# The last feed-forward's gate and up as block products: 20 f-tiles in seven products instead of eight, with weight sums on GpSimd

## The chip, the cores and the metric

The kernel runs on one core of a Trainium2 chip. The metric is the device time of one launch in microseconds; the median of several runs is given. Six parts of the core matter here: TensorE (PE in the rows; its weight loads are PEld), VectorE (DVE), ScalarE (ACT), GpSimd (POOL), SyncE (SP), which issues the DMAs, and the 16 DMA engines.

## The reference, cut to what matters

Three transformer layers over 512 tokens of width 1024, in float32. The change touches only the last feed-forward, at the end of the third layer:

```python
# second_block; D_MODEL = 1024, D_FF_2 = 2816, h is (1, 512, 1024)
u = rmsnorm(h, norm2_w[l]) * (1.0 + sc2) + sh2
ff = (jax.nn.silu(u @ w_ffn_gate[l]) * (u @ w_ffn_up[l])) @ w_ffn_down[l]
h = h + g2 * ff
...
return rmsnorm(h, final_norm_w)
```

## The kernel before

Features lie on the 128 partitions and the 512 tokens on the columns, so a product of a 128 x 128 weight tile with a k-tile of the operand gives 128 outputs x 512 tokens, one PSUM bank. A float32 product is made of three float32r matmuls (`mm3`, L533): weight high part x operand high part, high x low, low x high; a high part is a cast on ScalarE (`whi`, `xh`, `ph`), a low part the difference on VectorE (`wlo`, `xl`, `pl`).

The weights come as one stream in the order of `weight_plan` (L57): 16 tiles of 128 x 128 make a unit of 1 MB, loaded by one DMA of SyncE (`load_unit`, L424) into one of `RAWBUFS` = 2 raw buffers `wraw`. A unit is split in two halves of 1024 columns (`prep_half`, L477; `finish`, L443) into rings of three `whi` and three `wlo` tiles. The next unit is loaded when both halves of the one in its buffer are split (`load_ahead`, L469).

Code is emitted by a planner written out by hand (`Core.run`, L354): generators are threads with priorities, the planner keeps a clock for every engine from its own prices, and a thread runs when what it waits for is there by these clocks. The order on each engine is the order of emission; at run time every engine works through its own list in that order, and semaphores hold an instruction until its operands are made or its target is free.

The last feed-forward is `ffn("F2", ...)` (L862). There are 22 f-tiles of 128 hidden features, in two halves of 11; each half is followed by its part of the down product (8 output tiles of 11 k-tiles). The first f-tile's gate and up and the second one's gate are one wide product (`gemm_wide`, L555): three outputs side by side, first over tokens 0 to 255, then 256 to 511, while the operand is still being made by `explicit_x` (L1389). That one makes `ut` from the norm, then `xh` on ScalarE and `xl` on VectorE, for every third k-tile on GpSimd. Every other f-tile is a gate product and an up product (`gemm_a`, L541), 8 k-tiles of 3 matmuls of 512 columns each, then `act_chain` (L865): Silu on ScalarE into `fs`, multiply on VectorE, split into `ph` and `pl`, the operand of the down product. `update` (L598) adds a down product to `h`.

## Time and profile before

| | us |
|---|---|
| three runs | 1958.1, 1958.9, 1957.89 |
| median | 1958.1 |
| span of the profiled execution | 1956.9 |
| TensorE busy | 1940.5 |
| VectorE busy | 1139.1 |
| ScalarE busy | 843.1 |
| GpSimd busy | 7.0 |

The last feed-forward takes the end of the span: the wide product ends at 1595 us, the first half's gate and up at 1701, the second half's run from 1761 to 1885. The rows that are quoted further down have times in microseconds from the start of the span. A matmul is named by what it writes and reads (`ps<-xh,whi`), by its weight tile (128*128), and by partitions x columns; matmuls overlap, so their pitch is read from the starts. A bracket behind a row is the idle time of the engine ahead of it and what ended it. The granted TensorE clock is given as a share of 2.4 GHz.

### The profile page before, as it was taken

The page shows a single profiled execution, that of the slowest core. Times are in us where ns is not written, and L with a number is a line of the kernel's source. Part 1 is how long each engine was busy: PE and PEld are TensorE (multiplying, and loading weights), DVE is VectorE, ACT ScalarE, POOL GpSimd, SP SyncE. Part 2 cuts the span into 40 slices and gives each one's busy share as a digit, 9 for nine tenths or more (in the row PEclk, how much of TensorE's full clock was granted, in tenths as well). Part 3 has the DMA queues.
Part 4 walks back from the last instruction along what each step waited for, and adds up shares of the span by engine and source line. Part 5 has one row for each costly group of instructions (what it writes and reads, how often), then busy time and mean ns, then how long its engine had stood idle before and what let it go on. Part 6 is the DMA issues. An engine that isn't in the chain of part 4 may idle for free.

```text
span 1956.9 us, 23731 instructions
## 1 busy us (share of the span) xinstructions
PE 1940.5 (99%) x9331; PEld 1593.4 (81%) x9331; DVE 1139.1 (58%) x1946; ACT 843.1 (43%) x1361; POOL 7.0 (0%) x14
## 2 busy tenths in 40 slices
PE   9999999999999999999999999999999999999998
PEld 6888888888778878878888888898888888888887
DVE  5877865655665578887443344474777563333334
ACT  4866743322333466665322223352546352212233
POOL 0000000000000000000000000000000000000000
PEclk9999999999999999999999999999999999999999
DMA  6333224544442344431322222222121222222221
GB/s 192 99 85 97 76 86 176 194 178 172 185 170 86 123 130 128 126 114 65 108 94 99 87 108 87 104 84 97 54 82 44 87 87 86 99 95 89 106 86 65
DMA packets 48303, 211.94 MB, mean 108 GB/s; under 512 B 7056, under 2 KB 10304, under 8 KB 29248
## 3 DMA queue, kind: packets, MB, share of 16 engines
q1 hardware_dynamic: 48192, 210.43, 31.7%
q8 instruction: 73, 1.20, 0.2%
q14 instruction: 38, 0.31, 0.0%
HBM read 186.26 MB, written 2.10 MB: 96 GB/s over the span
## 4 chain that ended last, share of the span: by engine, by line
PE 96%; DVE 2%; DMA 1%; ACT 1%; issue 0%; SPq 0%; POOLq 0%; POOL 0%; DVEq 0%; ACTq 0%
PE ps L229 94%; PE ps L235 2%; DMA wraw<-wst 0%; DVE wlo L260 0%; DMA h<-xT 0%; DVE xl L276 0%; ACT xh L242 0%; DVE ut L276 0%; SPq L298 0%; ACT whi L242 0%; DVE h L260 0%; ACT sqh L242 0%; ACT ut L242 0%; DVE h L276 0%; DVE e L276 0%
## 5 line engine op out<-in xcount | busy, mean ns | idle before, releaser
L229 PE MATMUL ps<-xh,whi 128*128 128x512 f32 (+1 forms) x1856 | 728.7, 393 | 3.5 <-ACT whi L242 2.0
L229 PE MATMUL ps<-xh,wlo 128*128 128x512 f32 (+1 forms) x1856 | 722.4, 389 | 0.5 <-DVE wlo L260 0.5
L229 PE MATMUL ps<-xl,whi 128*128 128x512 f32 (+1 forms) x1856 | 719.3, 388 | 2.1 <-POOL xl L264 1.9
L242 ACT ACTIVATE whi<-wraw 128x1024 fp32r<-128x1024 f32 (+1 forms) x280 | 290.8, 1039 | 626.3 <-PE ps L229 579.6
L260 DVE TENSOR_TENSOR wlo<-wraw,whi 128x1024 fp32r<-128x1024 f32 (+1 forms) x280 | 335.6, 1199 | 337.1 <-ACT whi L242 334.3
L229 PEld LDWEIGHTS ps<-xh,whi 128*128 128x128 f32 x1856 | 348.8, 188 | 82.0 <-ACT whi L242 3.8
L229 PEld LDWEIGHTS ps<-xl,whi 128*128 128x128 f32 x1856 | 348.9, 188 | 80.6 <-POOL xl L264 2.9
L229 PEld LDWEIGHTS ps<-xh,wlo 128*128 128x128 f32 x1856 | 348.4, 188 | 78.8 <-DVE wlo L260 1.6
L229 PE MATMUL ps<-ph,whi 128*128 128x512 f32 (+1 forms) x572 | 214.2, 374 | 0.0
L229 PE MATMUL ps<-pl,whi 128*128 128x512 f32 (+1 forms) x572 | 213.3, 373 | 0.0
L229 PE MATMUL ps<-ph,wlo 128*128 128x512 f32 (+1 forms) x572 | 213.2, 373 | 0.0
L229 PEld LDWEIGHTS ps<-ph,wlo 128*128 128x128 f32 x572 | 107.7, 188 | 19.1
L229 PEld LDWEIGHTS ps<-ph,whi 128*128 128x128 f32 x572 | 107.7, 188 | 19.0
L229 PEld LDWEIGHTS ps<-pl,whi 128*128 128x128 f32 x572 | 107.7, 188 | 18.9
L260 DVE TENSOR_TENSOR fu<-ps,rb 128x512 f32<-128x512 f32 x44 | 30.4, 690 | 102.5 <-PE ps L229 102.5
L260 DVE TENSOR_TENSOR h<-ps,h 128x512 f32<-128x512 f32 (+1 forms) x82 | 49.8, 621 | 61.9 <-PE ps L229 59.8
L242 ACT ACTIVATE fs<-fg 128x512 f32<-128x512 f32 x44 | 27.8, 631 | 91.0 <-DVE fg L260 91.0
L260 DVE TENSOR_TENSOR fs<-ps,fs 128x512 f32<-128x512 f32 x22 | 15.2, 692 | 73.7 <-PE ps L229 73.0
L242 ACT ACTIVATE ph<-fs 128x512 fp32r<-128x512 f32 x66 | 41.8, 633 | 28.8 <-DVE fs L260 28.8
L276 DVE SCALAR_TENSOR_TENSOR adacc<-adaw,sc,adacc 128x1024 f32<-128x1024 f32 x42 | 53.7, 1279 | 0.0
L242 ACT ACTIVATE e<-e 128x1024 f32<-128x1024 f32 (+1 forms) x48 | 41.3, 905 | 21.7 <-DVE e L269 21.6
L242 ACT ACTIVATE s<-s,md 128x256 f32<-128x256 f32 (+3 forms) x80 | 45.9, 585 | 9.8 <-DVE md L269 8.4
(211 smaller groups left out, 1977.6 us busy)
## 6 DMA issues: line engine op xcount, KB each, us to landing
wraw<-wst SPq DMA_DIRECT2D x148, 1024.0 KB, 4.7
adaw<-wada SPq DMA_DIRECT2D x48, 512.0 KB, 5.7
qhh<-hin SPq DMA_DIRECT2D x32, 128.0 KB, 2.4
rfs<-rf SPq DMA_DIRECT2D x64, 64.0 KB, 2.0
khh<-rf SPq DMA_DIRECT2D x32, 128.0 KB, 2.5
h<-xT SPq DMA_DIRECT2D x8, 256.0 KB, 4.9
kst<-hin SPq DMA_DIRECT2D x16, 128.0 KB, 2.4
kst<-qkf SPq DMA_DIRECT2D x16, 128.0 KB, 2.4
```

The lines of the kernel that those rows point to most:

```text
L229: self.nc.tensor.matmul(out, lhsT, rhs, start=start, stop=stop, skip_group_check=not group)
L235: self.nc.tensor.transpose(out, in_, ident)
L242: self.nc.scalar.activation(out, in_, func, **kw)
L260: self.nc.vector.tensor_tensor(out, a, b, op)
L276: self.nc.vector.scalar_tensor_tensor(out, a, s, b, op0, op1)
```

## The change

From the third f-tile on (9 in the first half, 11 in the second) gate and up of one f-tile are one product of blocks. The 16 weight tiles of an f-tile are one unit: its four blocks of 512 columns are a11 (gate, k-tiles 0 to 3), a12 (gate, 4 to 7), a21 (up, 0 to 3) and a22 (up, 4 to 7). The operand has four blocks as well: k-tiles 0 to 3 and 4 to 7, tokens 0 to 255 (c1) and 256 to 511 (c2). Instead of eight block products there are seven, by Winograd's form of Strassen's scheme, with the weight blocks a11, a12, a22 and the sums s1 = a21 + a22, s2, s3 and s4. A block product is 4 k-tiles x 3 passes of 256 columns, 12 matmuls, so an f-tile has 84 of 256 columns instead of 48 of 512.

The sums of weight blocks are four GpSimd additions of 128 x 512 for each f-tile (`sums`), three of them in place in the raw unit. Seven blocks are split (cast on ScalarE, difference on VectorE) with 512 columns each into a ring of ten slots (`split_highs`, `split_lows`): six are the old `whi` and `wlo`, now one tile of six slots each, four are new (`whx`, `wlx`). The operand's blocks and their sums are made once (`blocks`): 16 GpSimd additions of 256 columns that put high and low part together again, sums and differences on VectorE (`d00` and so on), and their high and low parts (`th`, `tl`, and in `xh`, `xl` in place). The outputs are put together in `chain`: copies out of PSUM on ScalarE, additions on VectorE, then Silu, multiply and split as before. Product s2 is written into the bank that holds a11 and a12, and so waits for the flag c1, which an addition on VectorE sets; s3, a22 and s4 wait for c2, c3 and c4.

Besides, there are three raw buffers instead of two, the stream is filled up to whole units ahead of the third layer and behind each down product of the last feed-forward, and the DMA descriptors' scratch has a size of its own. The planner's work is the same elsewhere, but the third buffer shifts some of its order in layer 1.

```diff
-RAWBUFS = 2
+RAWBUFS = 3
...
+    def fill():
+        while len(tiles) % UNIT:
+            tiles.append(None)
+    def ffn(g, u, d, wide=False, seven=False):
         for half in range(2):
             for f in range(half * HALF, (half + 1) * HALF):
                 if wide and f == 0:
                     wide_k((g, 0), (u, 0), (g, P))
                     continue
+                if seven and f > 1:
+                    sevens.append(len(tiles) // UNIT)
                 if not wide or f != 1:
                     form_a(g, [f])
                 form_a(u, [f])
             form_a(d, range(8), nk=HALF, k0=half * HALF)
+            if seven:
+                fill()
...
     ffn("w_gate1", "w_up1", "w_down1")
+    fill()
...
+    ffn("w_ffn_gate_2", "w_ffn_up_2", "w_ffn_down_2", True, True)
...
+    hi_slots = wpool.tile([P, 6, 512], FR, name="whi")
+    lo_slots = wpool.tile([P, 6, 512], FR, name="wlo")
+    slots = [(hi_slots[:, i, :], lo_slots[:, i, :]) for i in range(6)]
...
+    EARLY = 2
+    BLOCK = {"a11": 0, "a12": 1, "a21": 2, "a22": 3, "s3": 2, "s2": 0, "s4": 1}
...
+    def steps_of(n):
+        steps = [(x, f) for f in range(EARLY) for x in ("a11", "a12")]
+        steps += [(x, f) for x in ("s1", "s2", "s3") for f in range(EARLY)]
+        steps += [(x, f) for f in range(EARLY - 1) for x in ("a22", "s4")]
+        for f in range(EARLY, n - 1):
+            steps += [("a11", f), ("a12", f), ("s1", f), ("s2", f), ("a22", f - 1), ("s4", f - 1), ("s3", f)]
+        f = n - 1
+        steps += [("a11", f), ("a12", f), ("s1", f), ("s2", f), ("a22", f - 1), ("s3", f), ("s4", f - 1), ("a22", f),
+                  ("s4", f)]
+        return steps
...
+        g["ring"] = [first, first + 1, *more, *((first + x) % 6 for x in range(2, 6))]
...
+    def sums(u0):
+        g = groups[u0]
+        for f in range(g["n"]):
+            u = u0 + f
+            if u not in raw:
+                yield lambda: u in raw
+            if f >= 2:
+                yield from got(f"W{u - 2}s1")
+            t = g["s1"][u] = g["pool"].tile([P, 512], FT, name="s1", bufs=2)
+            b = [raw[u][:, i * 512:(i + 1) * 512] for i in range(4)]
+            yield E._ready("pool_t", [t], b[2:]) - 1.0
+            E.ptt(t, b[2], b[3], OP.add)
+            E.set(f"W{u}S1")
+            yield from got(*(f"W{u}{x}" for x in (("a11", "a12") if f else ())))
+            if not f:
+                while highs.get(2 * u) or lows.get(2 * u):
+                    yield lambda: not (highs.get(2 * u) or lows.get(2 * u))
+            E.ptt(b[2], b[0], b[2], OP.add)
+            E.set(f"W{u}S3")
+            yield E.pool_t - 1.0
+            E.ptt(b[0], t, b[0], OP.add)
+            E.set(f"W{u}S2")
+            yield E.pool_t - 1.0
+            E.ptt(b[1], b[0], b[1], OP.add)
+            E.set(f"W{u}S4")
...
+    def seven(u0, name, f, out, x, fresh):
+        g, u = groups[u0], u0 + f
...
+        else:
+            yield from E.get(f"W{u}{name}x")
+            hi, lo = slots[g["slot"][name, f]]
+        for j in range(4):
+            c = slice(j * P, (j + 1) * P)
+            a, b = yield from x(j)
+            yield from E.there(hi[:, c], lo[:, c], a, b)
+            mm3(out, (hi[:, c], lo[:, c]), (a, b), fresh and j == 0, True, T // 2, False)
+            yield
+        taken[g["slot"][name, f]] = None
...
+    def ffn_seven(tag, pool, explicit, upd, split=False):
+        n = T // 2
+        c1, c2 = HALVES
+        tt = [pool.tile([P, 3, 4, n], FR, name=f"t{x}") for x in "hl"]
...
+        def blocks(j):
+            b = {}
+            for t in range(2):
+                for k in (j, j + 4):
+                    yield from E.get(f"{tag}x{k}_{t}")
+                    b[k // 4, t] = value[k][:, t, :]
+                    c = HALVES[t]
...
+                    d = E.ptt(b[k // 4, t], xh[:, k, c].bitcast(FT), xl[:, k, c].bitcast(FT), OP.add, n=n)
+            u, e, q, v = made[j][0][:, 0, :], made[j][0][:, 1, :], made[j][1][:, 0, :], made[j][1][:, 1, :]
+            def split(hi, lo, t, flag):
+                yield max(E.act_t - SLACK, E._ready("act_t", [hi], [t]))
+                yield E.act(hi, t, AF.Copy, n=n)
+                E.set(f"{tag}x{flag}{j}", E.tt(lo, t, hi.bitcast(FT), OP.subtract, n=n))
+            def minus(hi, lo, t, flag):
+                yield max(E.act_t - SLACK, E._ready("act_t", [hi], [t]))
+                yield E.act(hi, t, AF.Copy, scale=-1.0, n=n)
+                E.set(f"{tag}x{flag}{j}", E.stt(lo, t, -1.0, hi.bitcast(FT), OP.mult, OP.subtract, n=n))
+            yield d
+            E.tt(e, b[1, 1], b[0, 1], OP.subtract, n=n)
+            yield E.tt(u, b[0, 0], b[0, 1], OP.subtract, n=n)
+            E.spawn(after(f"{tag}k{j}", split(xh[:, j, c2], xl[:, j, c2], u, "s1")), 5)
+            yield E.tt(q, b[0, 0], e, OP.add, n=n)
+            E.spawn(minus(tt[0][:, 0, j, :], tt[1][:, 0, j, :], q, "s2"), 6)
+            yield E.tt(v, q, b[1, 0], OP.subtract, n=n)
+            E.spawn(split(tt[0][:, 1, j, :], tt[1][:, 1, j, :], e, "s3"), 8)
+            yield from split(tt[0][:, 2, j, :], tt[1][:, 2, j, :], v, "a22")
...
+        def chain(half, u, f, a, r5):
+            r = ps[:, a, c1]
+            yield from E.get(f"W{u}pa12")
+            g = pool.tile([P, T], FT, name="fs", bufs=3)
+            v = pool.tile([P, n], FT, name="fv", bufs=3)
+            d = E.act(g[:, c1], r, AF.Copy, n=n)
+            yield d
+            d = E.tt(g[:, c1], ps[:, a, c2], g[:, c1], OP.add, n=n)
+            E.set(f"W{u}c1", d)
+            yield d
+            E.act(g[:, c1], g[:, c1], AF.Silu, n=n)
+            yield from E.get(f"W{u}ps2")
+            E.set(f"W{u}c2", E.act(g[:, c2], r, AF.Copy, n=n))
+            yield from E.get(f"W{u}ps3")
+            d = E.act(v, r, AF.Copy, scale=-1.0, n=n)
+            E.set(f"W{u}c3", d)
+            yield d
+            b = yield from got(f"W{u}ps1")
+            E.set(f"W{u}c4", E.tt(v, v, ps[:, r5[0], c1], OP.subtract, n=n))
+            yield from E.get(f"W{u}pa22")
+            E.stt(g[:, c1], r, -1.0, g[:, c1], OP.mult, OP.mult, n=n)
+            E.release([a])
+            yield from E.get(f"W{u}ps4")
+            d = E.tt(g[:, c2], ps[:, r5[0], c1], g[:, c2], OP.add, n=n)
+            E.release([r5[0]])
+            yield d
+            yield E.act(g[:, c2], g[:, c2], AF.Silu, n=n)
+            d = E.tt(g[:, c2], g[:, c2], v, OP.mult, n=n)
+            if half:
+                yield from E.get(f"{tag}d{f}")
+            yield d
+            if not half:
+                hold(f)
...
+            for name, f in groups[u0]["steps"]:
+                u = u0 + f
+                f += 0 if half else 2
+                if name == "a11":
+                    a = (yield from E.alloc())[0]
+                    banks[f] = [a, []]
+                    E.spawn(chain(half, u, f, a, banks[f][1]), 4)
+                elif name == "s1":
+                    banks[f][1] += yield from E.alloc()
+                before = {"s2": "c1", "s3": "c2", "a22": "c3", "s4": "c4"}.get(name)
+                if before:
+                    yield from E.get(f"W{u}{before}")
+                a, r5 = banks[f]
+                out = {"a12": (a, c2), "s1": (r5, c1), "s4": (r5, c1)}.get(name, (a, c1))
+                b = out[0][0] if isinstance(out[0], list) else out[0]
+                yield from seven(u0, name, u - u0, ps[:, b, out[1]], operand(name), name in ("a11", "s1"))
+                E.set(f"W{u}p{name}", E.now())
...
+        skip_to_unit()
...
+            yield from ffn_seven("F2", pool, True, down("Z", x=False, scale=mod_col(5)), split=True)
...
+    nc = bacc.Bacc("TRN2", target_bir_lowering=False, num_devices=1, dynamic_dma_scratch_size=1024)
...
```

**How the order moves.** VectorE in the second half, around the f-tile whose hidden tile is number 4. Before, an f-tile has two weight splits of 1024 columns, the multiply (`fs`) and the hidden tile's low part (`pl`):

```order
L260 TENSOR_TENSOR wlo_13598<-wraw_13513,whi_13597 128x1024
L260 TENSOR_TENSOR fs_13630<-ps_69,fs_13630 128x512
L260 TENSOR_TENSOR wlo_13626<-wraw_13513,whi_13625 128x1024
L260 TENSOR_TENSOR pl4_12125<-fs_13630,ph4_12114 128x512
L260 TENSOR_TENSOR wlo_13661<-wraw_13576,whi_13660 128x1024
L260 TENSOR_TENSOR fs_13693<-ps_69,fs_13693 128x512
```

After, from the addition behind s4 of one f-tile (`fs_13904`, with the PSUM operand) to the addition that sets c1 of the f-tile two further on (`fs_14142`):

```order
L269 TENSOR_TENSOR fs_13904<-ps_69,fs_13904 128x256
L269 TENSOR_TENSOR wlo_85<-wraw_13931,whi_84 128x512
L269 TENSOR_TENSOR fs_13904<-fs_13904,fv_13905 128x256
L269 TENSOR_TENSOR fv_14024<-fv_14024,ps_69 128x256
L269 TENSOR_TENSOR wlo_85<-s1_13995,whi_84 128x512
L269 TENSOR_TENSOR pl4_12487<-fs_13904,ph4_12486 128x512
L269 TENSOR_TENSOR wlo_85<-wraw_13931,whi_84 128x512
L269 TENSOR_TENSOR fs_14142<-ps_69,fs_14142 128x256
```

The splits are half as wide and more, and ahead of the addition that s2 waits for stand the splits of a12, of s1 and of s2 of the next f-tile and the low part of the hidden tile of the one before.

GpSimd in the same place; before, nothing of GpSimd stands there. After, two f-tiles' units:

```order
L273 TENSOR_TENSOR s1_13995<-wraw_13931 128x512
L273 TENSOR_TENSOR wraw_13931<-wraw_13931 128x512
L273 TENSOR_TENSOR wraw_13931<-s1_13995,wraw_13931 128x512
L273 TENSOR_TENSOR wraw_13931<-wraw_13931 128x512
L273 TENSOR_TENSOR s1_14114<-wraw_14050 128x512
L273 TENSOR_TENSOR wraw_14050<-wraw_14050 128x512
```

In a unit's four rows come s1, s3, s2 and s4, the last three in place, so s3 and s2 follow the splits of the blocks that they write over.

VectorE at the end of the wide product, where the last operands are made. Before:

```order
L276 SCALAR_TENSOR_TENSOR ut_12339<-ps_69,gv_83,h_70 128x256
L260 TENSOR_TENSOR wlo_12309<-wraw_11902,whi_12308 128x1024
L276 SCALAR_TENSOR_TENSOR xl_72<-ut_12339,mod_77,xh_71 128x256
L276 SCALAR_TENSOR_TENSOR ut_12346<-ps_69,gv_83,h_70 128x256
L276 SCALAR_TENSOR_TENSOR xl_72<-ut_12346,mod_77,xh_71 128x256
L260 TENSOR_TENSOR wlo_12352<-wraw_12076,whi_12351 128x1024
L260 TENSOR_TENSOR fs_12387<-ps_69,fs_12387 128x512
```

After, to the low part of the last operand (`xl_72<-ut_11891`):

```order
L285 SCALAR_TENSOR_TENSOR xl_72<-ut_11882,mod_77,xh_71 128x256
L285 SCALAR_TENSOR_TENSOR ut_11891<-ps_69,gv_83,h_70 128x256
L269 TENSOR_TENSOR d01_11659<-b0_11650,d00_11658 128x256
L269 TENSOR_TENSOR d10_11660<-b5_11655,b1_11651 128x256
L269 TENSOR_TENSOR d10_11660<-b1_11651 128x256
L269 TENSOR_TENSOR d01_11659<-d01_11659,b4_11654 128x256
L269 TENSOR_TENSOR wlo_85<-wraw_11442,whi_84 128x1024
L269 TENSOR_TENSOR wlx_11649<-wraw_11612,whx_11648 128x512
L269 TENSOR_TENSOR d20_11662<-b6_11656,b2_11652 128x256
L269 TENSOR_TENSOR d20_11662<-b2_11652 128x256
L269 TENSOR_TENSOR d11_11661<-b1_11651,d10_11660 128x256
L285 SCALAR_TENSOR_TENSOR xl_72<-ut_11891,mod_77,xh_71 128x256
```

Two weight splits and seven steps on the operand's blocks now stand ahead of the last operand's low part; before, the low part followed its `ut` at once.

ScalarE at the end of the second half, where the down product's first weights are split. Before:

```order
L242 ACTIVATE whi_13940<-wraw_13828 128x1024
L242 ACTIVATE ph9_12119<-fs_13945 128x512
L242 ACTIVATE whi_13975<-wraw_13891 128x1024
L242 ACTIVATE fs_14008<-ps_69 128x512
L242 ACTIVATE whi_14003<-wraw_13891 128x1024
L242 ACTIVATE ph10_12120<-fs_14008 128x512
L242 ACTIVATE whi_14038<-wraw_13954 128x1024
```

After (`fs_14497` and `ph9` belong to the last f-tile but one, `fs_14609` and `ph10` to the last):

```order
L251 ACTIVATE fs_14609<-ps_69 128x256
L251 ACTIVATE fs_14609<-fs_14609 128x256
L251 ACTIVATE fs_14609<-ps_69 128x256
L251 ACTIVATE fv_14610<-ps_69 128x256
L251 ACTIVATE fs_14497<-fs_14497 128x256
L251 ACTIVATE ph9_13080<-fs_14497 128x512
L251 ACTIVATE whi_84<-wraw_14407 128x1024 x2
L251 ACTIVATE whi_84<-wraw_14542 128x1024
L251 ACTIVATE fs_14609<-fs_14609 128x256
```

The first casts of the down weights (1024 columns) now follow `ph9`; before, they were spread between the last f-tiles' steps.

## Rows read from the trace of the kernel before

**Rows 1.** Page, parts 1 and 4: engines' busy time, chain of waits by engine.

```profile
PE 1940.5 (99%) x9331; PEld 1593.4 (81%) x9331; DVE 1139.1 (58%) x1946; ACT 843.1 (43%) x1361; POOL 7.0 (0%) x14
...
PE 96%; DVE 2%; DMA 1%; ACT 1%; issue 0%; SPq 0%; POOLq 0%; POOL 0%; DVEq 0%; ACTq 0%
```

**Rows 2.** Windows of both gate-and-up stretches: start:end, length, busy by engine, clock, DMA.

```profile
1600.80:1701.40 100.60, 100.60 (x433) 80.93 (x432) 33.71 (x36) 28.40 (x36) 0.00 (x0) 1.00 0.27 96
1761.20:1884.20 123.00, 123.00 (x529) 98.95 (x528) 40.63 (x43) 34.20 (x43) 0.00 (x0) 1.00 0.26 94
```

**Rows 3.** Timeline (start, duration, engine, operation): TensorE, first and last of 528.

```profile
1761.37 0.40 PE L229 MATMUL ps<-xh,whi 128*128 128x512 f32 x1
...
1884.58 0.40 PE L229 MATMUL ps<-ph,whi 128*128 128x512 f32 x1
```

**Rows 4.** Timeline of TensorE at the end of the wide product.

```profile
1592.09 0.28 PE L229 MATMUL ps<-xh,wlo 128*128 128x256 f32 x1
...
1594.00 0.28 PE L229 MATMUL ps<-xh,whi 128*128 128x256 f32 x1
...
1595.09 0.39 PE L229 MATMUL ps<-xh,whi 128*128 128x512 f32 x1
```

**Rows 5.** Lines by form: operation, count | busy us, mean ns | idle before, releasers.

```profile
L242 ACT ACTIVATE whi<-wraw 128x1024 fp32r<-128x1024 f32 x272 | 287.6, 1058 | 625.7 <-PE ps L229 579.6 <-issue 42.6 <-DMA wraw<-wst 2.5
L242 ACT ACTIVATE ph<-fs 128x512 fp32r<-128x512 f32 x66 | 41.8, 633 | 28.8 <-DVE fs L260 28.8
L242 ACT ACTIVATE wh<-ps 128x256 fp32r<-128x256 f32 x20 | 7.6, 381 | 0.5 <-PE ps L229 0.5
L242 ACT ACTIVATE xh<-ut 128x256 fp32r<-128x256 f32 x8 | 3.3, 418 | 0.3
L260 DVE TENSOR_TENSOR wlo<-wraw,whi 128x1024 fp32r<-128x1024 f32 x272 | 332.2, 1222 | 336.9 <-ACT whi L242 334.1 <-PE ps L229 1.0
L260 DVE TENSOR_TENSOR h<-ps,h 128x256 f32<-128x256 f32 x20 | 7.3, 415 | 5.4 <-PE ps L229 3.7 <-PE ps L235 1.8
```

**Rows 6.** Timeline of VectorE: a split of 512 columns and the operation behind it.

```profile
403.80 0.68 DVE L260 TENSOR_TENSOR pl<-fs,ph 128x512 fp32r<-128x512 f32 x1
404.41 1.22 DVE L260 TENSOR_TENSOR adal<-adacc,adah 128x1024 fp32r<-128x1024 f32 x1
```

**Rows 7.** Timeline of GpSimd and VectorE while the last feed-forward's operand is made.

```profile
1581.76 0.73 POOL L264 TENSOR_TENSOR xl<-ut,xh 128x256 fp32r<-128x256 f32 x1 [3.30 <-ACT xh L242]
...
1582.55 0.48 DVE L276 SCALAR_TENSOR_TENSOR xl<-ut,mod,xh 128x256 fp32r<-128x256 f32 x1
...
1586.89 0.74 POOL L264 TENSOR_TENSOR xl<-ut,xh 128x256 fp32r<-128x256 f32 x1 [4.40 <-ACT xh L242]
1587.18 0.72 DVE L276 SCALAR_TENSOR_TENSOR xl<-ut,mod,xh 128x256 fp32r<-128x256 f32 x1 [1.19 <-ACT xh L242]
...
1590.01 1.21 DVE L260 TENSOR_TENSOR wlo<-wraw,whi 128x1024 fp32r<-128x1024 f32 x1
1590.93 0.88 POOL L264 TENSOR_TENSOR xl<-ut,xh 128x256 fp32r<-128x256 f32 x1 [3.30 <-ACT xh L242]
1591.22 0.87 DVE L276 SCALAR_TENSOR_TENSOR xl<-ut,mod,xh 128x256 fp32r<-128x256 f32 x1
```

**Rows 8.** Timeline of ScalarE and VectorE: the wide product's last operand.

```profile
1592.52 0.51 ACT L242 ACTIVATE xh<-ut,mod 128x256 fp32r<-128x256 f32 x1 [1.34 <-DVE ut L276]
1592.94 1.04 ACT L242 ACTIVATE whi<-wraw 128x1024 fp32r<-128x1024 f32 x1
1593.07 0.48 DVE L276 SCALAR_TENSOR_TENSOR xl<-ut,mod,xh 128x256 fp32r<-128x256 f32 x1 [0.58 <-ACT xh L242]
```

**Rows 9.** Page, part 6: a weight unit's DMA, count, KB, median us to landing.

```profile
wraw<-wst SPq DMA_DIRECT2D x148, 1024.0 KB, 4.7
```

**Rows 10.** Windows of the first 100 us and of a stretch of layer 1.

```profile
0.00:100.00 100.00, 95.95 (x462) 74.31 (x463) 69.74 (x93) 65.68 (x96) 0.52 (x5) 1.00 0.49 147
1200.00:1300.00 100.00, 98.81 (x549) 85.69 (x548) 51.25 (x87) 39.80 (x62) 2.30 (x3) 1.00 0.25 89
```

More of the change, by code (lines that the diff above doesn't have):

```diff
@@ L59, in weight_plan @@
     gains = {}
+    sevens = []
     def gain(name, width, i0):
@@ L901, in ffn @@
             last = KT - 2 if half and split else KT
+            for m in range(last):
+                b = yield from E.alloc()
+                hook = (lambda k: E.set(f"{tag}d{k}", E.now())) if m == KT - 1 else None
+                yield from gemm_a(b[0], take(HALF), lambda k: (ph[k], pl[k]), nk=HALF,
+                                  need=f"{tag}p{half}_" if m == 0 else None, hook=hook)
+                E.spawn(upd(m, b[0], half), 3)
+            if last == KT:
+                continue
+            i = take((KT - last) * HALF)
```

188 lines of the change are left out of this document (173 added, 15 removed).

## The prediction

> **What bounds the kernel now.** I read the page's busy shares and chain first: TensorE is busy 1940.5 us of a span of 1956.9 us and holds 96% of the chain that ended last [rows 1]. In the stretches by stage, the two gate-and-up stretches of the last feed-forward show no microsecond without TensorE, at a granted clock of 1.00 (the 2.4 GHz level), while VectorE and ScalarE are busy a third of the time and GpSimd not at all [rows 2]. So nothing but matmul time is to be won there, and what the change adds to the other engines is free only as long as it stays behind the matmuls.
>
> How fast matmuls follow each other comes from the timeline. In the second half's gate and up, 11 f-tiles of 48 matmuls of 512 columns start between 1761.37 and 1884.58 us [rows 3]: 123.21 / 528 = 0.2334 us each, 11.20 us for an f-tile. Matmuls of 256 columns, each with its own weights and the next operand already there, start 25 between 1592.09 and 1595.09 us [rows 4]: 0.1200 us each, more than half of 0.2334.
>
> **The saving.** Each of 20 f-tiles (9 in the first half, 11 in the second) loses its 48 wide matmuls and gets 7 products of 4 k-tiles and 3 passes, 84 matmuls of 256 columns: 84 x 0.1200 = 10.08 us. That is 1.12 us less, **22.4 us** in all. The same rate is the first thing to check in the new trace.
>
> **What the other engines get.** Per f-tile VectorE has seven low splits of 512 columns, one for the hidden tile, five 256-column steps. Back to back, 512 columns take it 0.61 us (403.80 to 404.41) [rows 6], 256 columns 0.42 alone [rows 5], in a row some 0.35 (less the 0.07 between 0.68 and 0.61): about 6.7 us. ScalarE gets eight casts at 0.63, three PSUM copies at 0.38 and two Silus at 0.42 [rows 5]: 7.0 us. GpSimd gets four sums of 512 columns. Its only row of that kind is 256 columns in 0.73 us [rows 7]; 512 lie between 0.73 + 0.43 = 1.16 (only the reading grows) and 1.46. I take 1.16, since the next paragraph shows the reading apart from the rest; 4.6 us. None of these fills 10.08 us.
>
> **The port.** But VectorE and GpSimd do not run beside each other freely. A VectorE operation with two operands in SBUF takes 0.48 us undisturbed and 0.72 us when issued 0.29 us after a GpSimd sum began; behind a 1024-column split, and with a GpSimd sum issued 0.29 us ahead of it, it takes 0.87 us, and the GpSimd sum itself 0.88 instead of 0.73 [rows 7]. One waits for the other. In the first case VectorE is let in 0.53 us after the sum began (1587.18 + 0.24 - 1586.89), in the second it loses 0.39: GpSimd keeps it out for about 0.43 us in 256 columns. For 512 the bounds are 0.43 and 0.86; both operands are read to the end, so I take 0.86. That a VectorE step with one operand in PSUM is not held off is assumed. Per f-tile, eight and a half VectorE operations (5.2 us) and four sums (3.4 us) share that way in: 8.6 of 10.08 us. It fits on average; the places where it must not be late are the question.
>
> The Trainium skill speaks against this change here. Its page "SBUF — State Buffer", section "Who interferes with whom", says that a VectorE instruction with two SBUF inputs contends with a GpSimd instruction that reads SBUF, and that the winner keeps the shared pair for the whole instruction. The trace agrees on the contention (0.72 for 0.48), but not on the whole instruction: 0.43 of 0.73 us. What the whole would cost is the slower rival.
>
> **Term C, the wait inside each f-tile.** The product s2 adds to the bank that holds a11 and a12, so it waits until these were taken out (ScalarE, then an add on VectorE, the last of the rows of VectorE's order). Only s1 lies between: 12 x 0.12 = 1.44 us. Unhindered it is enough: tail of a matmul 0.16 (0.28 less 0.12), copy 0.38, add 0.42, hand-overs of 0.04 (ScalarE's end at 1593.03 to VectorE at 1593.07) [rows 4, 5, 8]: 1.1 us. Hindered: take time zero at the end of a12. The slot for the split of a12 two f-tiles on is free after four products, 5.76 + 0.20; cast 0.63, low split 0.68 with 0.3 behind GpSimd's sum s2: over at 7.6. From there, in VectorE's order, come the multiply (0.35), the split of s1, the hidden tile's and the split of s2 (0.61 each), and GpSimd, freed by that same a12 split, puts s4, and s1 and s3 of the next unit, between them (0.86 each): 4.76 us through one door, until 12.36. The add must be issued at 10.08 + 1.44 - 0.46 = 11.06: 1.3 us late. If the third sum loses to the split of s2, 0.86 less: 0.4 late. In [rows 7] the one that waited first got in, which speaks for 1.3; a tenth or two in GpSimd's hand-overs turns it round. I take the mean, 0.86, on the 11 f-tiles whose add has two later sums ahead of it: **+9.5 us**, bounds 0 and 14. Behind the waiting add stand the splits of the f-tile's own a22 and s4, eight products ahead of TensorE, so they cost nothing. The unit that feeds these sums lands 4.7 us after its issue [rows 9], at about 8 us, before GpSimd asks for it.
>
> **Term A, the end of the wide product.** Now the last operand follows its ScalarE cast at once (1592.52, 1593.07), and only then the split of the next half starts (1592.94) [rows 8]; TensorE uses it at 1594.00. The new order puts, ahead of that cast, a 1024-column cast that waits for TensorE to have passed k-tile 5, and two of 512; and on VectorE a 1024 split, a 512 split and seven small steps ahead of the operand's low part. From the start of k-tile 5: three matmuls, their tail and a hand-over 0.56 + 1.06 + 1.22 + 0.61 + three steps 1.0 + 0.48 = 4.9, against 2.16 us of matmuls for k-tiles 5 and 6: 2.7 us at least. The operand sums on GpSimd add up to 0.9 at k-tile 5 (a 1024 split holds its low part off) and 0.9 more at the end. I take **+4 us**, bounds 2.7 and 5.
>
> **Term B, the first two f-tiles.** From the last operand to the second f-tile's add, VectorE has 12 operations of 512 and 24 of 256 columns: 12 x 0.61 + 24 x 0.36 = 16 us, in 16.8 us of matmuls (up of f-tile 1, 5.6; seven products, 10.1; 1.1 before). Alone it just fits. Seven sums and one operand sum of GpSimd in that time keep it out for 6.4 us, 5.6 too many. Nearly all its operations there have two SBUF operands, so nearer the upper end: **+4 us**, bounds 0 and 6.
>
> **Term D, the ends of both groups.** The order of ScalarE puts the first split of the down weights behind the hidden tile of the last f-tile but one. From the end of that tile's s4: 0.16 + add 0.42 + Silu 0.42 + multiply 0.42 + cast 0.63 + split 1.06 and 1.22, hand-overs 0.2: 4.5 us, with two products (2.88) left. 1.6 us, twice: **+3 us**, bounds 1 and 4.
>
> The rest at nothing, with 2 us either way: a third raw buffer and half a unit of empty tiles shift the order of layer 1's attention; TensorE idles 4.1 us in the first 100 and 1.2 us in the stretch from 1200 to 1300 [rows 10], so little is to be gained outside.
>
> **The sum.** -22.4 + 9.5 + 4 + 4 + 3 = -1.9 us. The profiled execution spans 1956.9 us; the median of the three runs is 1958.1, 1.2 above, which I take for what lies around a span. 1956.9 + 1.2 - 1.9 = **1956 us**: the saving is real and nearly all of it is given back in waits.
>
> **Rivals.**
> *The port decides nothing (faster).* GpSimd's sums fall into VectorE's gaps, so C and B are 0, and A and D stay at 2.7 and 3. For it: 8.6 of 10.08 us, and splits stand eight products ahead. Against: the stretched rows [rows 7], and the add at the end of the queue. 1958.1 - 22.4 + 5.7 = 1941 us.
> *GpSimd keeps VectorE out longer (slower).* If a 512-column sum holds it off for its whole 1.16 us, each of the three sums ahead of the add costs 0.3 more: 2.2 us late, x 11 = 24; B 8, A 5, D 3: 40 against 22.4, 1976 us. It decides from a hold of some 0.9 us on: there C passes 1.04 us for an f-tile and the sum turns positive. By the page named above this is what happens. Against it: 0.43 of 0.73 us.
> *It does not do what it says.* At 11.20 / 84 = 0.133 us for a narrow matmul no product is won and the waits stay: 1958.1 + 20.5 = 1979 us. Against it 0.1200 over 25 matmuls beside a working VectorE [rows 4, 8].
>
> **How the numbers follow.** My forecast (C between its two orders, 1948 to 1965) has 0.55, the faster rival 0.23, the slower 0.17, the last 0.05. A measurement of this kernel can tell 0.2% (3.9 us) from no change: below 1954.2 is faster, above 1962 slower. The forecast's 0.55 splits 0.17 faster, 0.30 same, 0.08 slower. So faster 0.40, same 0.30, slower 0.30. The range runs from the faster rival's time to short of the slower one's: 1941 to 1970, with about 0.07 below and 0.13 above left out.
>
> **What would show it.** Narrow matmuls 0.120 apart in products, and nearly no gap but ahead of s2, ended by VectorE's add, 0.4 to 1.3 us in 11 f-tiles; low splits of 0.68 us stretched to over 1 beside GpSimd; GpSimd sums near 1.2 us; 4 us of gap before the wide product's last k-tile, 4 in the first seven products after it, 1.6 before each down product, ended by the split. Adds on time, or sums of 1.5 us and more, would make it wrong, as would a gap ended by GpSimd itself.

## The result, and the profile after

The changed kernel takes 2001.5 us (median of 4 runs, 1997.1 to 2004.1) against 1958.0 for the kernel before (4 runs): a ratio of 1.0218, 95% interval 1.0203 to 1.0232. It is slower by 43.5 us where 2 us less were forecast, outside the range of 1941 to 1970. The profiled execution spans 2002.4 us, 45.5 more than before's.

The page's parts 1 and 4 of the changed kernel answer to [rows 1], and the two gate-and-up stretches to [rows 2]:

```profile
PE 1944.6 (97%) x10051; PEld 1636.3 (82%) x10051; DVE 1281.9 (64%) x2156; ACT 910.1 (45%) x1555; POOL 138.9 (7%) x110
...
PE 86%; DVE 8%; issue 2%; ACT 1%; DMA 1%; POOL 1%; SPq 0%; DVEq 0%; ACTq 0%; POOLq 0%
```

```profile
1600.80:1702.00 101.20, 84.37 (x590) 81.52 (x591) 84.40 (x117) 48.80 (x105) 46.60 (x33) 0.88 0.21 74
1781.00:1898.00 117.00, 100.18 (x712) 97.04 (x711) 94.94 (x111) 52.59 (x109) 60.16 (x40) 0.90 0.21 73
```

Two things are new in the second fence. TensorE, without a gap before, is idle for 17 us of each stretch, and its granted clock is 0.88 and 0.90 where it was 1.00. TensorE's waits from 1570 to 1900 us (total us, times, longest) say for whom, first before and then after:

```profile
PE ps L229 <- POOL xl L264: 1.0, 3, 0.4
```

```profile
PE ps L238 <- DVE fs L269: 27.4, 14, 4.2
PE ps L238 <- DVE xl L285: 10.6, 2, 10.0
PE ps L238 <- POOL xl L273: 1.2, 3, 0.4
```

The addition that sets c1 (`fs`) and the wide product's last operand (`xl`): the two places that the prediction named. The steady state on TensorE, in the second half; each row is the first matmul of an s2:

```profile
1829.13 0.39 PE L238 MATMUL ps<-th,whx 128*128 128x256 f32 x1 [1.93 <-DVE fs L269]
...
1842.88 0.39 PE L238 MATMUL ps<-th,whi 128*128 128x256 f32 x1 [1.93 <-DVE fs L269]
...
1856.63 0.39 PE L238 MATMUL ps<-th,whi 128*128 128x256 f32 x1 [1.94 <-DVE fs L269]
```

An f-tile takes 13.75 us instead of 11.20 before and 10.08 in the prediction's sum. 2.09 of that is the wait: 1.93 us idle, and from start to start the row is 2.21 behind the matmul before it, where 0.12 would do. Windows behind the third of these rows (PE busy and its matmul count stand first, the clock third from the end) show more:

```profile
1857.00:1858.00 1.00, 1.00 (x8) 1.00 (x7) 0.60 (x2) 0.54 (x2) 0.00 (x0) 0.55 0.00 0
1858.00:1861.00 3.00, 3.00 (x18) 3.00 (x18) 0.96 (x2) 0.91 (x2) 0.00 (x0) 0.58 0.52 150
1861.00:1865.00 4.00, 4.00 (x36) 4.00 (x35) 3.21 (x6) 2.41 (x6) 1.58 (x2) 1.00 0.37 154
```

After the pause the clock goes down to half, the 1.2 GHz level, for some 3.4 us, and TensorE has 18 matmuls in 3 us; behind that, at 1.00, 36 in 4. At the lower level the starts tell the pitch, nine matmuls from the first of these rows to the second:

```profile
1858.14 0.41 PE L238 MATMUL ps<-th,wlo 128*128 128x256 f32 x1
...
1860.06 0.41 PE L238 MATMUL ps<-th,wlo 128*128 128x256 f32 x1
```

That is 0.213 us each instead of 0.120. Sixteen of them in 3.4 us lose 1.5 us, and 13.75 - 10.08 - 2.09 = 1.58 us is what the f-tile has left for it.

Why the addition is late, in VectorE's rows between two s2 of the second half, from the split of a12 to the addition, and GpSimd's in the same time:

```profile
1822.10 1.23 DVE L269 TENSOR_TENSOR wlo<-wraw,whi 128x512 fp32r<-128x512 f32 x1 [0.18 <-ACT whi L251]
...
1823.59 0.40 DVE L269 TENSOR_TENSOR fv<-fv,ps 128x256 f32<-128x256 f32 x1
1823.92 1.44 DVE L269 TENSOR_TENSOR wlo<-s,whi 128x512 fp32r<-128x512 f32 x1
1825.29 1.78 DVE L269 TENSOR_TENSOR pl<-fs,ph 128x512 fp32r<-128x512 f32 x1
1826.99 1.75 DVE L269 TENSOR_TENSOR wlo<-wraw,whi 128x512 fp32r<-128x512 f32 x1
1828.66 0.41 DVE L269 TENSOR_TENSOR fs<-ps,fs 128x256 f32<-128x256 f32 x1
```

```profile
1821.48 1.30 POOL L273 TENSOR_TENSOR wraw<-s,wraw 128x512 f32<-128x512 f32 x1 [8.24 <-DVE wlo L269]
1823.48 1.34 POOL L273 TENSOR_TENSOR wraw<-wraw 128x512 f32<-128x512 f32 x1 [0.69 <-DVE wlo L269]
1824.78 1.74 POOL L273 TENSOR_TENSOR s<-wraw 128x512 f32<-128x512 f32 x1
1826.60 1.59 POOL L273 TENSOR_TENSOR wraw<-wraw 128x512 f32<-128x512 f32 x1
```

Add start and duration. The four GpSimd sums end at 1822.78, 1824.82, 1826.52 and 1828.19; the four VectorE splits end at 1823.33, 1825.36, 1827.07 and 1828.74, each 0.54 or 0.55 us later. A split of 512 columns that meets a sum gets in only when the sum is over, and `pl`, which reads nothing that GpSimd writes, fares no better than the others. The whole stretch of 1570 to 1900 us says the same. Of the 63 VectorE operations of 512 columns with two SBUF operands that start inside a GpSimd operation, 0.3 us or more ahead of its end, 62 end 0.54 to 0.56 us after it, and all 20 of 256 columns 0.28 or 0.29; the one other goes ahead of a sum that was itself waiting, and that sum takes 2.18 us. From start to start the four take 5.9 us instead of the 2.4 of four in a row [rows 6], and TensorE stands still for it.

### The profile page after: what moved, and what is told of

Same layout as the page of the kernel before. It is cut to its first block, busy times and chain, and to the rows that moved or that the text cites. A ratio compares the mean times of both kernels' runs of the same rounds, so it can differ in the third digit from the quotient of the medians.

```text
span 2002.4 us, 25792 instructions
## 1 busy us (share of the span) xinstructions
PE 1944.6 (97%) x10051; PEld 1636.3 (82%) x10051; DVE 1281.9 (64%) x2156; ACT 910.1 (45%) x1555; POOL 138.9 (7%) x110
## 4 chain that ended last, share of the span: by engine, by line
PE 86%; DVE 8%; issue 2%; ACT 1%; DMA 1%; POOL 1%; SPq 0%; DVEq 0%; ACTq 0%; POOLq 0%
PE ps L238 85%; DVE wlo L269 2%; PE ps L244 2%; DVE pl L269 1%; DVE wlx L269 1%; DVE fs L269 1%; ACT whi L251 1%; DVE d L269 1%; POOL wraw L273 0%; DVE xl L285 0%; DMA wraw<-wst 0%; DVE s L290 0%; SPq L307 0%; DVE fv L269 0%; DVE xl L269 0%
## 5 line engine op out<-in xcount | busy, mean ns | idle before, releaser
L238 PE MATMUL ps<-xl,whi 128*128 128x512 f32 (+1 forms) x1712 | 644.1, 376 | 13.3 <-DVE xl L285 10.8
L238 PE MATMUL ps<-xh,whi 128*128 128x512 f32 (+1 forms) x1712 | 654.5, 382 | 2.2 <-DVE fv L269 0.9
L238 PE MATMUL ps<-xh,wlo 128*128 128x512 f32 (+1 forms) x1712 | 644.5, 376 | 1.1 <-DVE wlo L285 0.6
L269 DVE TENSOR_TENSOR wlo<-wraw,whi 128x1024 fp32r<-128x1024 f32 (+2 forms) x312 | 357.0, 1147 | 265.9 <-ACT whi L251 264.3
L251 ACT ACTIVATE whi<-wraw 128x1024 fp32r<-128x1024 f32 (+2 forms) x312 | 293.0, 944 | 469.7 <-PE ps L238 440.0
L238 PEld LDWEIGHTS ps<-xl,whi 128*128 128x128 f32 x1712 | 322.8, 189 | 75.8 <-DVE xl L285 12.7
L238 PEld LDWEIGHTS ps<-xh,wlo 128*128 128x128 f32 x1712 | 322.2, 188 | 65.8 <-DVE wlo L269 1.1
L238 PEld LDWEIGHTS ps<-ph,whi 128*128 128x128 f32 x572 | 107.7, 188 | 20.4 <-ACT whi L251 1.7
L238 PE MATMUL ps<-th,whi 128*128 128x256 f32 x156 | 50.3, 323 | 15.0 <-DVE fs L269 13.7
L269 DVE TENSOR_TENSOR pl<-fs,ph 128x512 fp32r<-128x512 f32 x66 | 57.2, 867 | 3.3 <-ACT ph L251 3.1
L273 POOL TENSOR_TENSOR wraw<-wraw 128x512 f32<-128x512 f32 x40 | 58.0, 1449 | 12.3 <-DVE wlo L269 6.2
```

What stands on the lines that cost most here:

```text
L238: self.nc.tensor.matmul(out, lhsT, rhs, start=start, stop=stop, skip_group_check=not group)
L251: self.nc.scalar.activation(out, in_, func, **kw)
L269: self.nc.vector.tensor_tensor(out, a, b, op)
L273: self.nc.gpsimd.tensor_tensor(out, a, b, op)
```

## The experiments

Theory 1, the door: a GpSimd sum keeps VectorE's operations with two SBUF operands out until it ends; the late addition is what TensorE waits for, and the pause is what brings the clock down. Theory 2, the queue: VectorE simply has too much ahead of that addition, whoever makes the sums. Theory 3: the clock falls because of the narrow products.

**Without the weight sums.** In `sums` the four GpSimd operations go, so the gate and up of these f-tiles are not those of the reference; s1 is read from a21 as it is.

```diff
-            E.ptt(t, b[2], b[3], OP.add)
+            t = g["s1"][u] = b[2]
...
-            E.ptt(b[2], b[0], b[2], OP.add)
...
-            E.ptt(b[0], t, b[0], OP.add)
...
-            E.ptt(b[1], b[0], b[1], OP.add)
```

> The changed kernel without the four GpSimd sums of each f-tile (the blocks are used as they come, so the last feed-forward's gate and up are wrong; splits, products and chain stay; the 16 operand sums on GpSimd stay too). Theory 1, the door: each 512-column sum keeps VectorE out until it ends, 1.1 us, and that makes the addition ahead of s2 late. Then the waits ahead of s2 (2.0 to 2.1 us in 11 f-tiles) go to under 0.2, the clock stays at 1.00 in both stretches behind the wide product, the wide product's stall falls from 10 to some 5 us, and the time is 1958 - 22.4 + 5 + some 5 at the first f-tiles and the ends = 1945 us. Theory 2, the queue: VectorE simply has too many operations ahead of that addition; then the waits stay above 1 us and the time above 1975. Theory 3, the narrow products themselves pull the clock down: the waits go, the clock still falls to 0.88, and the time is near 1965.

1946.4 us, ratio 0.9937 (0.9922 to 0.9951). No wait ahead of any s2 is left, and the clock is 1.00 in both stretches. Theory 2 falls: the same queue, without the sums, is on time. Theory 3 falls too: the same narrow products run at full clock. TensorE waits 1.8 us for the wide product's last operand instead of 10.0; two waits of 1.5 and 1.2 us ahead of that are left as well, near the 5 us in all that had been expected.

**The sums on VectorE.** `E.ptt` becomes `E.tt` in `sums`, and the planner's times are VectorE's.

> The changed kernel with the weight sums on VectorE instead of GpSimd, everything else the same. VectorE gets four operations of 0.61 us more for each f-tile. Theory 1, the door: the four sums cost VectorE 2.4 us where GpSimd's kept it out for 4 x 1.1 = 4.4, so the addition ahead of s2 comes some 0.5 to 1 us late instead of 2.1, the clock falls rarely or not, and the time is 1958 - 22.4 + 11 x 0.8 + 8 = 1952 us (1945 to 1962). Theory 2, the queue: four more operations in VectorE's order ahead of and behind the addition make it later, waits of 3 us and more, the time above 2010.

1962.5 us, 1.0021 (1.0012 to 1.0031), 10 us above the 1952 expected and just above its range. The waits ahead of s2 are 0.3 to 1.0 us, as theory 1 has it; the starts cost more than expected (TensorE waited 2.2 and 1.6 us in the first block products, and the clock fell behind the first of these two). So the same sums cost VectorE less when it makes them itself than when GpSimd makes them for it.

**a12 in a bank of its own.** s2 then waits only for ScalarE's copy of a11.

```diff
-            yield from E.get(f"W{u}pa12")
+            yield from E.get(f"W{u}pa11")
...
-            d = E.act(g[:, c1], r, AF.Copy, n=n)
-            yield d
-            d = E.tt(g[:, c1], ps[:, a, c2], g[:, c1], OP.add, n=n)
-            E.set(f"W{u}c1", d)
+            E.set(f"W{u}c1", E.act(g[:, c1], r, AF.Copy, n=n))
+            yield from E.get(f"W{u}pa12")
+            d = E.tt(g[:, c1], ps[:, own[u], c1], g[:, c1], OP.add, n=n)
...
+                elif name == "a12":
+                    own[u] = (yield from E.alloc())[0]
...
-                out = {"a12": (a, c2), "s1": (r5, c1), "s4": (r5, c1)}.get(name, (a, c1))
+                out = {"a12": (own.get(u), c1), "s1": (r5, c1), "s4": (r5, c1)}.get(name, (a, c1))
```

> The changed kernel with the product a12 in a PSUM bank of its own, so that s2 waits only for ScalarE's copy of a11, which runs during a12, and no longer for the addition on VectorE; the sums stay on GpSimd. If the addition's place in VectorE's queue is what the waits come from, they go and the clock stays up: 1958 - 22.4 + 10.7 (wide product) + 4 + 4 = 1954 us. But by theory 1 VectorE has then 6.7 us of work and 4 x 1.1 us of shut door for each f-tile, 11.1 us against 10.08 of matmuls: it falls behind by 1 us for each f-tile and TensorE waits for low splits instead, some 1 us in 18 f-tiles, 1970 us, with the clock falling in some of them. Theory 2, the queue alone: 1954 us.

1969.8 us, 1.0056 (1.0039 to 1.0073). That is theory 1's time, and VectorE is full, as it said (57.5 of 60 us, in the windows two runs further down); but TensorE does not wait for low splits, as had been expected, and the clock does not fall in the steady f-tiles. The wait has moved and halved: s2 now waits 0.85 us for ScalarE's copy, which stands in ScalarE's queue behind a Silu that needs VectorE's addition. ScalarE's rows of this kernel, and TensorE's:

```profile
1834.31 0.42 ACT L251 ACTIVATE fs<-fs 128x256 f32<-128x256 f32 x1 [3.49 <-DVE fs L269]
1834.64 0.61 ACT L251 ACTIVATE whx<-wraw 128x512 fp32r<-128x512 f32 x1
1835.16 0.36 ACT L251 ACTIVATE fs<-ps 128x256 f32<-128x256 f32 x1
...
1835.57 0.38 PE L238 MATMUL ps<-th,whi 128*128 128x256 f32 x1 [0.85 <-ACT fs L251]
```

An f-tile takes 11.18 us (the first matmuls of s2 start at 1824.39 and 1835.57), near the 11.1 that the expectation gave for VectorE. At pauses of this length, 1.0 us from start to start, the clock stays at 1.00 in the second half.

**The change's other parts alone.** Three raw buffers, the padding, the slots and the scratch, with gate and up as before.

> The kernel before with the change's other parts alone: three raw buffers, the weight stream filled up to whole units ahead of the third layer, one tile of six slots for the splits, the smaller scratch; gate and up as before in eight products. The changed kernel's wide product starts 0.85 us earlier than before's, so all of this is worth 0.5 to 1.5 us: 1957 us. If these parts had a cost that the changed kernel's profile hides, it would be above 1960.

1959.2 us, 1.0003 (0.9994 to 1.0013). They cost and bring nothing that can be measured, where a gain of 0.5 to 1.5 us had been expected.

**Both: own bank, and the sums on VectorE.**

> The changed kernel with both edits of the two runs before: the weight sums on VectorE, and a12 in a PSUM bank of its own so that s2 waits only for ScalarE's copy of a11. Theory 1, the door: VectorE has 6.7 + 2.4 = 9.1 us of work in 10.08 us of matmuls and nothing that shuts it out, so the steady f-tiles run without a wait and at a clock of 1.00; left are the wide product's end (4.3 us with the sums on VectorE), the first f-tiles (4 to 5) and the ends (3): 1958.5 - 22.4 + 11.5 = 1948 us. If VectorE's queue alone decides (theory 2), the waits of 0.4 to 1.1 us of the run with the sums on VectorE stay, now ahead of other products: 1960 us.

1952.2 us, 0.9962 (0.9948 to 0.9975). The steady f-tiles run as theory 1 has it, without a wait. The same 60 us (VectorE is the third engine) of the kernel without weight sums, of the own-bank kernel with the sums on GpSimd, and of this one:

```profile
1800.00:1860.00 60.00, 60.00 (x503) 60.00 (x502) 41.28 (x75) 36.05 (x74) 0.00 (x0) 1.00 0.35 123
```

```profile
1800.00:1860.00 60.00, 55.12 (x449) 53.87 (x448) 57.47 (x74) 32.39 (x71) 29.61 (x20) 1.00 0.26 90
```

```profile
1800.00:1860.00 60.00, 60.00 (x503) 60.00 (x503) 54.94 (x102) 38.27 (x78) 0.00 (x0) 1.00 0.29 103
```

An f-tile takes 10.08 us in the first and third and 11.18 in the second, so 60 us hold 5.95, 5.37 and 5.95 of them, and VectorE is busy for 6.9, 10.7 and 9.2 us in each. The four sums cost VectorE 3.8 us when GpSimd makes them and 2.3 when it makes them itself. What the expectation left out, and missed by 4 us, is the clock behind the pauses that are left, at the wide product's end, in the first f-tiles and ahead of the last down product: 1-us windows from 1570 us on (busy time times the missing share of the clock) add up to 6.9 us of matmul time lost at the lower level.

**All of it, with the operand's sums later.** The blocks' differences and the first unit's splits are emitted once the last operand is made; the down product's first split is emitted behind the last f-tile's s2.

```diff
+        yield from E.get(f"F2x{KT - 1}_1")
         g = groups[u]
...
+            yield from E.get(f"{tag}x{KT - 1}_1")
             yield d
             E.tt(e, b[1, 1], b[0, 1], OP.subtract, n=n)
...
+                if name == "s2" and u == u0 + groups[u0]["n"] - 1:
+                    E.spawn(early(2 * u + 2), 899)
```

> As the run with own bank and the sums on VectorE, and besides: the sums and differences of the operand's blocks and the splits of the first unit are emitted only once the last operand of the wide product is made, and the down product's first weight split is emitted behind the last f-tile's s2 instead of behind its s4. Expected: the wide product's stall goes from 4.3 to some 1 us (as before), the ends from 3 to under 1, the first f-tiles lose 3 to 5 us because the operand sums now stand in their time: 1958.5 - 22.4 + 6 = 1942 us (1938 to 1948). If the operand sums only move the stall, the first f-tiles lose 8 and it is 1947.

1946.8 us, 0.9937 (0.9924 to 0.9949). In this kernel the early split takes the slot in which the last s4 of the second half still lies, so that product reads other weights; the number and kind of operations is the right one. The wide product's end and the ends of the groups are free of waits. But the stall moved: in the first f-tiles TensorE waits three times, 8.8 us more from start to start, while VectorE works without a pause from 1592 to beyond 1620 us. Of the two outcomes on record it is the second.

**From the fourth f-tile on.** The candidate: as the last one, with the early split put into slots that are free, and the third f-tile left in eight products, so that VectorE has 11.2 us in which little else is asked of it.

```diff
-                if seven and f > 1:
+                if seven and f >= 3:
...
+                state["pair"] = (state["pair"] + skip) % 3
```

> The candidate: own bank for a12, weight sums on VectorE, the operand's sums and differences emitted once the last operand is made, the down product's first weight split emitted earlier (into slots that are free by then), and the block products from the fourth f-tile on instead of the third: the third one stays in eight products, so that VectorE has 11.2 us with little else to do while it makes the operand's blocks. In the run before with these edits but the third f-tile, VectorE worked without a pause from 1592 to 1622 us and TensorE waited 8.8 us in the first f-tiles. Expected: those waits go to under 2 us, nothing at the ends, none in the steady f-tiles, the clock at 1.00: 19 x 1.12 = 21.3 us saved, 1 to 2 us of waits left: 1958.7 - 21.3 + 2 = 1939 us (1937 to 1944). If VectorE is still behind when the block products begin, waits of 4 to 5 us and a fall of the clock: 1946.

1937.2 us (1936.6 to 1938.4), 0.9888 (0.9871 to 0.9904): faster than both kernels. The second half's stretch has no gap and a clock of 1.00, and GpSimd nothing to do:

```profile
1761.00:1866.00 105.00, 105.00 (x872) 104.71 (x871) 90.67 (x165) 63.43 (x128) 0.00 (x0) 1.00 0.32 111
```

One wait of 0.7 us is left in the first f-tiles. 19 f-tiles x 1.12 = 21.3 us of saving, and 21.3 are measured (1958.6 less 1937.2). That the two meet is partly luck. In the profiled execution some 3 us are lost in the waits that are left and in a fall of the clock at 1577 us, in the wide product, and the wide product begins 1.8 us earlier than before's (1556.43 and 1558.26); the spans differ by 20.3.

**The pause without the products.** Two kernels with the arithmetic of the kernel before, in 512-column products, and a made gap ahead of 18 f-tiles: the gate product writes into the bank of the up product before it. One more copy on ScalarE was to lengthen it.

```diff
+                if f > 1 or half:
+                    yield E.act(s, s, AF.Copy)
...
+                    if explicit and one:
+                        yield from E.get(f"{tag}g{half}_{f - 1}")
+                        one = one[::-1]
+                        bg, bu = one
```

> The kernel before, gate and up in 512-column products, but with a gap made ahead of 18 f-tiles of the last feed-forward: the gate product writes into the bank that the up product of the f-tile before left, so it waits for Silu, one more copy of 512 columns on ScalarE and the multiply, some 2.1 us. It tells what the pause alone does to TensorE's clock, without narrow products and without GpSimd. If a pause of 2 us makes the clock fall for 3.4 us, as in the changed kernel, each gap costs 2.1 + 1.7 us: 1958.5 + 18 x 3.8 = 2027 us and the granted clock in the second half is near 0.88. If the clock falls only with the 256-column products, each gap costs 2.1: 1996 us at a clock of 1.00.

1979.1 us, 1.0101 (1.0083 to 1.012). The gap came out at half of what was meant, 0.85 us of idle time (1.02 from start to start), since Silu and the copy run beside the up product. It costs 18 x 1.02 = 18.4 of the 20.4 us, and the clock does not fall. That leaves open what a gap of 2 us does, so the gap was lengthened on VectorE, with two more multiplies of the same kind ahead of the real one:

```diff
+                for i in range(2 if f > 1 or half else 0):
+                    E.tt(again, ps[:, bu, :], s, OP.mult)
```

> The kernel before with a longer gap ahead of 18 f-tiles of the last feed-forward than in the run before (1.02 us there, at which the clock stayed): the multiply that frees the bank follows two more operations of the same kind on VectorE, 0.6 us each, so the gap is some 2.2 us, as long as the waits ahead of s2 in the changed kernel. Products of 512 columns, no GpSimd. If the length of the pause decides, the clock falls to 1.2 GHz for 3.4 us behind most gaps, each costs 2.2 + 1.7 us, and the time is 1958.7 + 18 x 3.9 = 2029 us. If it takes the narrow products, the clock stays at 1.00 and the time is 1958.7 + 18 x 2.2 = 1998 us.

2021.9 us, 1.0321 (1.0301 to 1.0342), between the two. TensorE's waits of the two kernels, the shorter gap first:

```profile
PE ps L229 <- DVE fs L260: 15.4, 18, 0.9
```

```profile
PE ps L229 <- DVE fs L260: 43.1, 18, 2.4
```

The longer gaps bring the clock down behind 8 of the 18 (the windows show it at some 0.5 for 3.4 us each time), without a narrow product and without GpSimd. In the changed kernel it falls behind all 11 steady waits, which are shorter. But there too it does not always fall: at 1624.82, in the first block products, a wait of 1.70 us leaves it at 1.00. So a pause of some 2 us can be enough to lose the clock, but not every time, and what decides it between 8 of 18 and 11 of 11 stays open.

**The door by itself.** The kernel before with four sums behind each f-tile's multiply, whose results nothing uses.

```diff
+                for i in range(4 if f > 1 or half else 0):
+                    E.ptt(dummy[i % 2], s, s, OP.add)
```

> The kernel before with four sums of 512 columns on GpSimd behind the multiply of each f-tile from the third on; nothing uses their results. It measures the door by itself. Theory 1: a GpSimd sum keeps VectorE's operations with two SBUF operands out until it ends; the hidden tile's low part (0.68 us alone) and the weight split that meet the sums end some 0.55 us (512 columns) or 1.1 us (1024) after the end of a sum, 1.4 to 1.8 us for the low part. As the recorded prediction had it, a sum holds only 0.86 of its 1.16 us and the low part takes at most 1.5. TensorE has cover in this kernel, so the time stays at 1958.5 to 1962 us in either case.

1958.1 us, 1.0002 (0.9992 to 1.0012): no cost, because TensorE is covered. VectorE is not. Its groups by form from 1610 to 1890 us:

```profile
L260 DVE TENSOR_TENSOR wlo<-wraw,whi 128x1024 fp32r<-128x1024 f32 x50 | 77.8, 1555 | 69.7 <-ACT whi L242 69.4
L260 DVE TENSOR_TENSOR pl<-fs,ph 128x512 fp32r<-128x512 f32 x20 | 30.5, 1524 | 0.0
L260 DVE TENSOR_TENSOR fs<-ps,fs 128x512 f32<-128x512 f32 x20 | 13.8, 691 | 70.7 <-PE ps L229 70.7
```

The hidden tile's low part, two SBUF operands, takes 1.52 us instead of 0.68 [rows 6]. By size alone this run does not tell the two holds apart: these sums read one tile twice and take 1.04 us alone, so both readings allow it. The ends do. A sum, and the low part that meets it:

```profile
1646.88 2.02 POOL L264 TENSOR_TENSOR dummy<-fs 128x512 f32<-128x512 f32 x1
```

```profile
1647.92 1.52 DVE L260 TENSOR_TENSOR pl<-fs,ph 128x512 fp32r<-128x512 f32 x1
```

1648.90 and 1649.45, 0.55 us apart as in the changed kernel, and so it is in all 20 of them. Nothing reads these sums, so it is no operand that VectorE waits for. The multiply `fs` keeps its 0.69, but it runs ahead of the sums. That an operation with one operand in PSUM is not held off, which the prediction assumed, shows in the changed kernel's groups from 1570 to 1900 us:

```profile
L269 DVE TENSOR_TENSOR fs<-fs,fv 128x256 f32<-128x256 f32 x16 | 8.8, 548 | 0.5 <-ACT fs L251 0.5
...
L269 DVE TENSOR_TENSOR fv<-fv,ps 128x256 f32<-128x256 f32 x17 | 6.9, 408 | 1.7 <-ACT fv L251 1.7
```

With both operands in SBUF 256 columns average 0.55 us; with one in PSUM they keep 0.41, although 13 of the 17 run inside a sum (as the one at 1823.59, in the fence of the result).

## Why the prediction was wrong

**The saving** was right, and the rival by which the change does not do what it says falls. At full clock the changed kernel's narrow matmuls follow each other as in [rows 4]:

```profile
1702.79 0.28 PE L238 MATMUL ps<-xh,whi 128*128 128x256 f32 x1
...
1707.11 0.28 PE L238 MATMUL ps<-th,whi 128*128 128x256 f32 x1
```

36 matmuls in 4.32 us, 0.1200 each. The candidate gets nearly all of it.

**The port** is the step that failed, at the sentence "VectorE is let in 0.53 us after the sum began (1587.18 + 0.24 - 1586.89)". It took the time by which the operation was stretched (0.24) as the time for which it stood at the door. But an operation has a start of its own before it needs the door, and that ran while it waited. The rows that were in hand say so when ends are compared instead of durations: in [rows 7] the sum ends at 1586.89 + 0.74 = 1587.63 and VectorE's operation at 1587.18 + 0.72 = 1587.90, 0.27 later; the next pair ends at 1591.81 and 1592.09, 0.28 later. That constant rest, 0.28 us for 256 columns and 0.55 for 512, is read here as the operation's own passage, which begins when the sum is over; the 0.13 us that are missing to 0.41 and 0.68 would be its start. The Trainium skill, page "SBUF — State Buffer", section "Who interferes with whom", calls the shared pair an exclusive lock and says, of VectorE's two-port modes, that whoever issues first keeps it for the whole instruction. The prediction set that aside with "0.43 of 0.73 us"; the trace agrees with the page, here for operations with two SBUF operands, by the ends above.

**GpSimd's sum** was put at 1.16 us, the lower end of 1.16 to 1.46; undisturbed it takes 1.28 to 1.30, and behind a VectorE split up to 1.74, because the door shuts both ways.

**Term C** followed in part from these two: 11 f-tiles with a wait of 1.9 to 2.1 us from start to start, 22.6 us together, where 9.5 stood with bounds of 0 and 14. The place and the count were right. From the a12 split to the addition VectorE took 6.56 us (1822.10 to 1828.66) where 4.76 and the split itself, 0.68 + 0.3, had been summed: 0.8 more. Some 0.5 of that is the door: by the starts, the a12 split takes 1.16 where 0.98 stood, and the three behind it 1.37, 1.70 and 1.67 where 0.61 + 0.86 = 1.47 stood. The other 0.33 is a step that the sum left out although VectorE's order shows it, `fv` between the multiply and the split of s1. And of its two orders, 1.3 and 0.4 us late, the prediction took the mean; 1.3 and 0.8 make the 2.1 that came. The slower rival had 2.2 us for each of the 11, with the hold right and `fv` left out as well, so its nearness is partly luck.

**Term A** was 4, with bounds of 2.7 and 5, and is 10.8, by the first matmul that reads the last operand's low part, before and after:

```profile
1594.12 0.28 PE L229 MATMUL ps<-xl,whi 128*128 128x256 f32 x1
```

```profile
1604.89 0.58 PE L238 MATMUL ps<-xl,whi 128*128 128x256 f32 x1 [9.98 <-DVE xl L285]
```

The rows of VectorE ahead of the last operand, with GpSimd's sums beside them:

```profile
1599.15 1.48 DVE L269 TENSOR_TENSOR d<-b,b 128x256 f32<-128x256 f32 x1
1600.55 1.48 DVE L269 TENSOR_TENSOR d<-b 128x256 f32<-128x256 f32 x1
1601.95 1.48 DVE L269 TENSOR_TENSOR d<-b,d 128x256 f32<-128x256 f32 x1
1603.35 1.48 DVE L285 SCALAR_TENSOR_TENSOR xl<-ut,mod,xh 128x256 fp32r<-128x256 f32 x1
```

```profile
1598.77 1.58 POOL L273 TENSOR_TENSOR wraw<-s,wraw 128x512 f32<-128x512 f32 x1 [1.89 <-DVE wlo L269]
1600.42 1.32 POOL L273 TENSOR_TENSOR wraw<-wraw 128x512 f32<-128x512 f32 x1
1601.71 1.44 POOL L273 TENSOR_TENSOR s<-wraw 128x512 f32<-128x512 f32 x1
1603.23 1.32 POOL L273 TENSOR_TENSOR wraw<-wraw 128x512 f32<-128x512 f32 x1
```

Steps of 0.41 to 0.48 take 1.48 because each has to let a whole weight sum pass. The prediction had counted the operand sums in this place but not the first two units' weight sums, which GpSimd starts as soon as those units are there. Without them that matmul starts at 1597.23, 3.1 us late, which is inside the prediction's bounds.

**Term B** was right in the first half (4.0 us against 4), but the second half begins in the same way, with two f-tiles' products at once, and loses 5.7 us that no term had. **Term D** was right in both groups together (2.9 against 3), though not in each: 1.0 and 1.9 where 1.6 had been summed.

**The clock** is the term that is missing altogether. [Rows 2] show 1.00 and no pause; nothing in the sum asked what the clock does when pauses come back every f-tile. 1-us windows of the changed kernel from 1570 us on, reckoned as above, give 22.6 us of matmul time lost at the lower level, as much as the whole saving. So even with the port right the sum would have been some 20 us short.

The sum as measured: -22.4 + 22.6 (C) + 10.8 (A) + 4.0 and 5.7 (B, both halves) + 2.9 (D) + 22.6 (clock) = 46.2 us, against 45.5 between the spans. The slower rival, 1976 us, had the waits nearly right (40 for 46.0); it too was without the clock.

## What to carry to other kernels

To see whether one engine shuts another out, compare the ends of the two operations, not how much one was stretched: a constant distance between the ends means that the whole other operation had to pass. Work given to GpSimd beside a VectorE that reads two SBUF operands is not free work: here four sums cost VectorE 3.8 us as GpSimd's and 2.3 as its own, so it was cheaper not to hand them over. And where a change puts pauses of about 2 us between matmuls, price each at its length plus what the clock may take behind it (here 1.6 us), and look first for a way to take the wait off the path, such as another PSUM bank.
